# Low parts of weight chunks by an accumulating DMA, and the closing sums of an SSM scan on VectorE

## The chip, the cores and the metric

The kernel runs on one core of one Trainium2 chip, with its TensorE (matrix products), VectorE, ScalarE, GpSimd and SyncE, a 128-partition on-chip memory and 16 DMA engines. The metric is the device time of one execution in microseconds; lower is better. In the profile the engines are called PE (with PEld for its weight loads), DVE, ACT, POOL and SP; a q behind the name (SPq, POOLq) is the engine's queue of instructions that only issue or wait.

## What is computed

One layer of a decoder block for 256 tokens of 2048 columns, in float32:

```python
u = RMSNorm(h)
q, k, v, s_in, g_a, g_s = split(u @ w_in)             # 1024, 1024, 1024, 1024, 2048, 2048 columns
y_a = diff_attention(q, k, v)                         # 8 heads, two softmax maps each
y_s = s5(s_in)                                        # 64 groups, complex state of 64, scan over tokens
y_s = gelu(y_s); y_s = y_s * sigmoid(y_s @ w_glu + b_glu)
merged = sigmoid(g_a) * (y_a @ Wa) + sigmoid(g_s) * (y_s @ Ws)
h = h + RMSNorm(merged @ w_out)
z = RMSNorm(h)
h = h + RMSNorm((silu(z @ w_gate) * (z @ w_up)) @ w_down)
```

## The kernel before

**Split products.** Each float32 weight and each activation is kept as a high part (rounded to the format float32r of TensorE) and a low part (what the rounding left). A product is three matmuls: x high by w high, x high by w low, x low by w high.

**Blocks and chunks.** The weights stream through in blocks. A block is 16 or 8 chunks of 128 rows by 1024 columns (512 KB). For a chunk there are 4 products of 128x512 (2 token tiles by 2 halves of the columns), so 12 matmuls. The blocks run in the order ssm (the SSM's input), q, k, v, ga0, ga1, wa0, wa1, gs0, gs1, then glu, ws0, ws1, wo0, wo1, eleven ffn blocks and down.

**The ring.** `do_load` (L178) loads a chunk on SP's queue into `raw`, of which there are 4 buffers. `do_split` (L191) makes `hi` with a copy on ScalarE (L205) and `lo` with a subtraction on VectorE (L206); there are 3 buffers each of `hi` and `lo` until the glu block. `ensure` (L210) writes the split of a chunk two chunks ahead of its matmuls and the loads a further four ahead. A load waits until its raw buffer is free, that is until `lo` of the chunk that held it has been made.

**Side work.** `prep` (the parameters of the SSM), `u_parts`, `ssm` and `attn` are Python generators in a list of tasks. After the matmuls of a chunk `pump` (L230) takes as much from them as the budget SIDE = 1.4 allows. The SSM works through 16 halves of groups (the loop at L723). For each half GpSimd builds the rotation tables tabC and tabS of the next one (six instructions, L635 to L640); TensorE brings B u into `side`; VectorE rotates it (ssA to ssD), scans it (four scans, L756 and L757) and rotates it back (four products, L762 to L767); GpSimd closes with a difference into `sre` (L764) and a sum into `sim` (L768). TensorE then multiplies these with C (`finish`, L672). The next half reuses ssA to ssD.

**The order.** Until the second chunk of the first block the instructions stay in the order of the program (`pin`). After that a scheduler that simulates the times when the kernel is built decides the order on each engine and puts in the waits; on the chip each engine then follows its fixed order. GpSimd also issues the DMAs of its own queue, in the same order as its other work.

**Memory.** `big8` (L142) gives tiles of 128x2048 from a pool of 6. `bb` holds the SSM's B in `prep` (L567 to L613) in two tiles of the pool mixp.

Of the kernel before, what the change touches and what calls it, by code (L numbers as in the profile page):

```python
# [9 lines left out]
F32 = mybir.dt.float32  # L10
# [16 lines left out]

SIDE = 1.4     # how much of the side work goes between two chunks of weights


class InOrder:
    """An engine whose instructions stay in the order of the program while pin[0] is set."""

# [12 lines left out]
class Block:  # L46
    """One pass of a weight stripe (nk k-tiles of 1024 columns) through the tensor engine."""

    def __init__(self, name, nk, load, lhs, evac, order=None, pre=None, post=None,
                 budget=0.0, alloc=None, mm=None, ensure=None, before=None):  # L50
        self.name, self.nk, self.load, self.lhs, self.evac = name, nk, load, lhs, evac
        self.order, self.pre, self.post, self.budget = order, pre, post, budget
        self.alloc, self.mm, self.ensure = alloc, mm, ensure
        self.before = before or {}


# [12 lines left out]
def token_order(nk, head=0, tail=0):  # L69
    """Token tile 0 before token tile 1 over the first `head` and the last `tail` chunks."""  # L70
    steps = []
    if head:
        for t in range(2):
            for k in range(head):
                steps.append([(k, t, c) for c in range(2)])
    else:
        steps.append([(0, t, c) for t in range(2) for c in range(2)])
        head = 1
    for k in range(head, nk - tail):
        steps.append([(k, t, c) for t in range(2) for c in range(2)])  # L80
    for t in range(2):
        if tail:
            for c in range(2):
                steps.append([(k, t, c) for k in range(nk - tail, nk)])
    return steps
# [3 lines left out]
def hybrid_block_kernel(  # L89
# [45 lines left out]
    def side4():  # L135
        """One bank out of the four, where nothing else needs two at once."""
        cyc["n"] += 1
        if cyc["n"] % 4 == 3:
            cyc["t"] = side2()
        return side() if cyc["n"] % 4 in (1, 2) else cyc["t"][:, 1 if cyc["n"] % 4 == 0 else 0, :]  # L140
# [7 lines left out]
    class Scratch:  # L148
        """Short-lived tiles, cut from a few of the large ones."""

# [21 lines left out]

# [1 line left out]
    flat = []  # L174
# [3 lines left out]
    def do_load(i):  # L178
        """Loads one chunk; late in the kernel some go in pairs into spare large tiles."""
        blk, k = flat[i]  # L180
        if late.get("ffn") and i % 8 in (4, 6):
            r = big8(shape=(P, 2, 1024))
            blk.load(k, r)
            raws[i], raws[i + 1] = r[:, 0, :], r[:, 1, :]
            return 2
        r = ring.tile([P, 1, 1024], F32, tag="raw", name=nm("raw"), bufs=4)
        blk.load(k, r)
        raws[i] = r[:, 0, :]
        return 1

    def do_split(i):  # L191
        blk, k = flat[i]
        if late and i % 5 >= 3:
            h = late["pool"].tile([P, 1024], F32R, tag="hi", name=nm("hi"), bufs=2)
            l = late["pool"].tile([P, 1024], F32R, tag="lo", name=nm("lo"), bufs=2)
        else:
            h = ring.tile([P, 1024], F32R, tag="hi", name=nm("hi"), bufs=3)
            l = ring.tile([P, 1024], F32R, tag="lo", name=nm("lo"), bufs=3)
        if i == 0:
            first_split(h, l, raws.pop(0))  # L200
            his[i], los[i] = h, l
            return
        if blk.ensure:
            blk.ensure(k)
        A.copy(h, raws[i])  # L205
        V.tensor_tensor(l, raws[i], h.bitcast(F32), op=ALU.subtract)  # L206
        his[i], los[i] = h, l
        del raws[i]
# [10 lines left out]
    def cap(blk, n, start=False):  # L219
        """The splits go no further than n chunks from the start of blk, for now."""  # L220
        state["cap"] = None if n is None else blk.base + n
# [89 lines left out]

# [1 line left out]
    ident = const.tile([P, P], F32, name="ident")  # L313
# [8 lines left out]

# [1 line left out]
    xT_h = tpool.tile([P, 16, S], F32R, tag="T16", name="xT_h")  # L324
# [29 lines left out]
    def warm_up(n):  # L354
        """Products without a use, which bring the tensor engine's clock up while the first data comes in."""
        for _ in range(n):
# [36 lines left out]
    def make_rstd(ss, n, tag, inv):  # L393
        """(sum of squares * inv + eps) ** -0.5 for [P, n]."""
        ms = const.tile([P, n], F32, name=nm(tag + "m"))
# [17 lines left out]

# [1 line left out]
    def dve_exp(dst, src, n, pool):  # L415
# [13 lines left out]
    def dve_sincos(s_out, c_out, th, n, pool):  # L429
# [32 lines left out]
        V.tensor_copy(nn, q.bitcast(I32))  # L462
        # quarter turns: cos = [1,0,-1,0], sin = [0,1,0,-1]
        V.tensor_scalar(a, nn, 2.0, None, op0=ALU.is_equal)
# [11 lines left out]

# [1 line left out]
    def prep():  # L478
# [36 lines left out]
        yield 2.0  # L515
        # -(exp(s1) - exp(s2) + lam_init)
        nlam = const.tile([P, 1], F32, name="nlam")
# [20 lines left out]
        yield from dve_sincos(fl(sn), fl(cs), fl(th), 256, pp)  # L538
        # coef = (a_bar - 1) / lam
        w = [pp.tile([P, 32], F32, name=nm("cw")) for _ in range(6)]  # L540
# [16 lines left out]
        yield 1.5  # L557
        # b_bar, [ (g p), h, pair ] from transposes of the rows
        bps = []
        for t_ in braw:  # L560
# [5 lines left out]
            yield 0.5  # L566
        bb = [mixp.tile([P, 32, 16], F32, name=nm("bb")) for _ in range(2)]  # L567
        bc = lambda c_: c_.unsqueeze(1).broadcast_to([P, 16, 32])
        tmp = [pp.tile([P, 16, 32], F32, name=nm("bt")) for _ in range(2)]
        for o, (c0, c1, op) in enumerate(((cre, cim, ALU.subtract), (cim, cre, ALU.add))):  # L570
# [3 lines left out]
            yield 1.8  # L574
        # rotation tables: e^{i theta b}, b < 16, and e^{i theta 16 a}, a < 16
        tabs = []
# [27 lines left out]
        yield 0.1  # L604
        # B as blocks for pairs of groups, transposed, in high and low parts
        bh, bl = (ga[:, i, :, :].rearrange("p a (c o q) -> p (a c) o q", c=4, o=2) for i in range(2))
# [18 lines left out]

# [1 line left out]
    def table(hh):  # L627
# [16 lines left out]
    def u_parts():  # L644
        """u transposed, and its high and low parts to where the products take them from."""
        un = hold["u"]
# [21 lines left out]
    def ssm():  # L668
# [38 lines left out]
        def bu_mm(hf):  # L707
            # u and B of two pairs of groups: [u high; u low; u high] against [B high; B high; B low]
            us, bs = hold.pop("stack")
# [13 lines left out]
        for hh in range(2 * NG):  # L723
# [39 lines left out]
            V.tensor_tensor(tC, tD, tss, op=ALU.mult)  # L763
            G.tensor_tensor(sre[:, 2 * hf:2 * hf + 2, :], tA, tC, op=ALU.subtract)  # L764
            yield 1.2
            V.tensor_tensor(tB, tB, tss, op=ALU.mult)
            V.tensor_tensor(tD, tD, tcs, op=ALU.mult)  # L767
            G.tensor_tensor(sim[:, 2 * hf:2 * hf + 2, :], tB, tD, op=ALU.add)  # L768
            yield 1.2
# [7 lines left out]
        for k in range(8):  # L777
            tc.keep_in_program_order(A.activation(uT[:, k, :], uT[:, k, :], AF.Gelu_apprx_tanh))
            yield 0.1
        # the table of the sigmoids that come next is loaded ahead of them  # L780
        tc.keep_in_program_order(A.activation(const.tile([P, 1], F32, name="presig"), half[:, :1], AF.Sigmoid))
# [4 lines left out]

# [1 line left out]
    def attn():  # L788
# [113 lines left out]

# [1 line left out]
    def lhs_of(th, tl):  # L904
# [32 lines left out]
    def first_split(h, l, raw):  # L937
        """The first chunk and the first two k-tiles of x, in the order in which they are used."""
        ps = x_transposes(0)
# [10 lines left out]

    # first block: transposes of x run one step ahead of their use
    xdone = [1]
# [74 lines left out]

    # GLU: the weights are stationary, so that the result comes out transposed
    def glu_pre():
# [53 lines left out]
    def m_transpose(hf):  # L1083
        """Transposes of the merged branches for one half of the columns."""
        if not mT:
# [142 lines left out]

# [1 line left out]
    def lz(k, t):  # L1230
# [52 lines left out]

    # the rest of the norm, four k-tiles of one token tile at a time, ahead of their use
    blocks[-NB].before = {
# [13 lines left out]

    # down: k-tile by k-tile, 2048 columns, all banks  # L1300
    hs = {}
# [32 lines left out]
    def dn_evac(key, accs):  # L1334
        # the two banks of one tile are read only once both are complete
        t, c = key
# [25 lines left out]
    def dn_finish(t, c0, n, eng=None):  # L1362
        """The last scaling, the residual and the store of n columns."""
        f, r, cs = hold["f"][t], hold["rf", t], slice(c0, c0 + n)
# [60 lines left out]
```

## Time and profile before

| what | value |
|---|---|
| median of the runs | 1446.54 us (1445.51 to 1448.1, 3 runs) |
| span of the profiled execution | 1444.7 us |
| PE busy | 1384.3 us, 96% of the span |
| DVE busy | 912.6 us, 63% |
| ACT busy | 670.7 us, 46% |
| POOL busy | 279.8 us, 19% |
| DMA moved | 266.69 MB, 185 GB/s in the mean |

The profiled execution lasted its span and what lies around it: the first instruction starts when the span starts, and the median of the runs is 1.8 us above the span. Matmuls overlap in TensorE's pipeline, so its busy time says only where it has nothing to do at all. The shares are means over stages with different limits; views of single stretches, given in microseconds from the start of the span, tell them apart. A granted clock of 1.00 is 2.4 GHz.

### The profile page before, as it was taken

What the parts mean: (1) busy time and instruction counts of PE and PEld (TensorE: products, weight loads), DVE (VectorE), ACT (ScalarE), POOL (GpSimd) and SP (SyncE); (2) the same over time, 40 slices, a digit from 0 to 9 for tenths busy, and PEclk for the clock granted to TensorE, in tenths of its full rate; (3) what the DMA queues carried; (4) which work ended last, traced back from release to release, by engine and by line L of the source; (5) the groups of instructions that cost most, each with busy time, mean ns of one, the idle gap of its engine ahead of it and who ended that gap; (6) DMA issues with size and microseconds to landing.
All of it is one profiled execution on the core that took longest, in us unless ns stands there. A gap on an engine that the chain in (4) does not pass through costs nothing.

```text
span 1444.7 us, 17345 instructions
## 1 busy us (share of the span) xinstructions
PE 1384.3 (96%) x6367; PEld 1123.6 (78%) x6367; DVE 912.6 (63%) x1114; ACT 670.7 (46%) x963; POOL 279.8 (19%) x227
## 2 busy tenths in 40 slices
PE   8999897899889899999999999999999999999997
PEld 6887665678667579888788888888888888888885
DVE  5965889978898876755764444444444445555555
ACT  4654343375533356444464444444444444444443
POOL 3293676501756620000000000000000000000001
PEclk9999899999989899999999999999999999999999
DMA  8688554445455466655576556466565555555651
GB/s 259 187 265 256 159 153 124 133 147 165 142 153 153 118 187 234 248 189 191 164 258 219 174 190 201 161 207 203 172 205 169 198 203 177 204 191 188 203 175 59
DMA packets 102005, 266.69 MB, mean 185 GB/s; under 512 B 10176, under 2 KB 17168, under 8 KB 98528
## 3 DMA queue, kind: packets, MB, share of 16 engines
q1 hardware_dynamic: 100704, 260.09, 55.7%
q10 hardware_dynamic: 608, 4.20, 0.8%
q0 software_dynamic: 608, 1.30, 0.4%
q8 instruction: 50, 0.82, 0.2%
q14 instruction: 35, 0.29, 0.1%
HBM read 257.16 MB, written 8.39 MB: 184 GB/s over the span
## 4 chain that ended last, share of the span: by engine, by line
issue 52%; PE 29%; DVE 11%; POOL 5%; DMA 1%; ACT 1%; SPq 0%; POOLq 0%; DVEq 0%; ACTq 0%
PE acc L41 27%; PE side L41 3%; DVE lo L41 3%; POOL sre L764 2%; DVE ssC L41 2%; DVE ssB L41 2%; DVE ssD L41 2%; DVE ssA L41 2%; POOL sim L768 1%; POOL tabS L638 1%; DMA b<-in_x_dram 1%; ACT hi L41 1%; DMA raw<-in_w_in_dram 0%; DVE b L41 0%; SPq L623 0%
## 5 line engine op out<-in xcount | busy, mean ns | idle before, releaser
L41 DVE TENSOR_TENSOR lo<-raw,hi 128x1024 fp32r<-128x1024 f32 (+1 forms) x341 | 439.2, 1294 | 242.5 <-ACT hi L41 237.5
L41 ACT CAST hi<-raw 128x1024 fp32r<-128x1024 f32 (+1 forms) x340 | 354.7, 1051 | 406.4 <-PE acc L41 327.1
L41 PE MATMUL acc<-lo,zT_h 128*128 128x512 f32 x704 | 274.9, 390 | 0.0
L41 PE MATMUL acc<-hi,zT_l 128*128 128x512 f32 x704 | 274.0, 389 | 0.0
L41 PE MATMUL acc<-hi,zT_h 128*128 128x512 f32 x704 | 270.9, 392 | 0.2 <-ACT zT_h L41 0.2
L41 DVE TENSOR_TENSOR lo<-b,hi 128x1024 fp32r<-128x1024 f32 x124 | 151.1, 1224 | 147.6 <-ACT hi L41 147.6
L41 PE MATMUL acc<-lo,xT_h 128*128 128x512 f32 x512 | 211.8, 417 | 15.6 <-DVE lo L41 15.6
L41 PE MATMUL acc<-hi,xT_l 128*128 128x512 f32 x512 | 207.1, 407 | 0.0
L41 ACT CAST hi<-b 128x1024 fp32r<-128x1024 f32 x124 | 130.5, 1053 | 120.4 <-PE acc L41 104.0
L41 PE MATMUL acc<-hi,xT_h 128*128 128x512 f32 x512 | 169.7, 411 | 3.9 <-ACT hi L41 3.5
L41 PEld LDWEIGHTS acc<-hi,zT_h 128*128 128x128 f32 x704 | 132.2, 188 | 27.7 <-ACT zT_h L41 0.7
L41 PEld LDWEIGHTS acc<-hi,zT_l 128*128 128x128 f32 x704 | 132.2, 188 | 27.6
L41 PEld LDWEIGHTS acc<-lo,zT_h 128*128 128x128 f32 x704 | 132.2, 188 | 26.6
L41 PEld LDWEIGHTS acc<-lo,xT_h 128*128 128x128 f32 x512 | 102.0, 199 | 43.7 <-DVE lo L41 21.0
L398 POOL TENSOR_TENSOR rstdf<-rstdfm,half 128x1 f32<-128x1 f32 x2 | 1.1, 546 | 691.6 <-DVE rstdfm L41 691.6
L41 PEld LDWEIGHTS acc<-hi,xT_h 128*128 128x128 f32 x512 | 99.3, 197 | 28.6 <-ACT hi L41 4.9
L41 PEld LDWEIGHTS acc<-hi,xT_l 128*128 128x128 f32 x512 | 101.7, 199 | 21.5 <-issue 0.8
L41 PE MATMUL acc<-hi,b 128*128 128x512 f32 x256 | 84.2, 404 | 0.8 <-DVE ga L41 0.6
L764 POOL TENSOR_TENSOR sre<-ssA,ssC 128x512 f32<-128x512 f32 x16 | 47.5, 2970 | 121.1 <-DVE ssC L41 121.1
L41 PE MATMUL acc<-lo,hTh 128*128 128x512 f32 x176 | 68.5, 389 | 0.0
L41 PE MATMUL side<-hi,hTh 128*128 128x512 f32 x176 | 68.5, 389 | 0.0
L41 PE MATMUL side<-lo,hTh 128*128 128x512 f32 x176 | 68.5, 389 | 0.0
(209 smaller groups left out, 1818.0 us busy)
## 6 DMA issues: line engine op xcount, KB each, us to landing
raw<-in_w_in_dram SPq DMA_DIRECT2D x127, 512.0 KB, 4.2
raw<-in_w_ffn_gate_dram SPq DMA_DIRECT2D x96, 256.0 KB, 2.8
raw<-in_w_ffn_up_dram SPq DMA_DIRECT2D x96, 256.0 KB, 3.0
raw<-in_w_ffn_down_dram SPq DMA_DIRECT2D x44, 512.0 KB, 3.7
b<-in_w_ffn_down_dram SPq DMA_DIRECT2D x22, 1024.0 KB, 4.9
b<-in_w_ffn_gate_dram SPq DMA_DIRECT2D x40, 512.0 KB, 3.8
b<-in_w_ffn_up_dram SPq DMA_DIRECT2D x40, 512.0 KB, 4.8
raw<-in_w_out_dram SPq DMA_DIRECT2D x32, 512.0 KB, 4.6
```

Of the source, the lines that this page charges most:

```text
L41: ins = f(*a, **kw)
L398: G.tensor_tensor(r, ms, half[:, :n], op=ALU.pow)
L638: G.tensor_tensor(tss, hi(sa), lo(cb), op=ALU.mult)
L764: G.tensor_tensor(sre[:, 2 * hf:2 * hf + 2, :], tA, tC, op=ALU.subtract)
L768: G.tensor_tensor(sim[:, 2 * hf:2 * hf + 2, :], tB, tD, op=ALU.add)
```

## The change

In the blocks q, k, v, ga, wa and gs each odd chunk gets its low part without VectorE. ScalarE makes hi as before, and it also writes minus the rounded weights into `lo`. A DMA on GpSimd's queue then adds `raw` to `lo` in place. `lo` of each fourth chunk (k % 4 == 3) has a buffer of its own, lo4. `bb` moves into a tile of `big8`, which frees the room for lo4. The two closing sums of the SSM's loop move from GpSimd to VectorE. Apart from comments that are dropped, this is all:

```diff
@@ class Block
+        self.dma_lo = name[:2] in ("q", "k", "v", "ga", "wa", "gs")
@@ do_split
             h = ring.tile([P, 1024], F32R, tag="hi", name=nm("hi"), bufs=3)
-            l = ring.tile([P, 1024], F32R, tag="lo", name=nm("lo"), bufs=3)
+            l = (small([P, 1024], "lo4", F32R) if blk.dma_lo and k % 4 == 3 else
+                 ring.tile([P, 1024], F32R, tag="lo", name=nm("lo"), bufs=3))
...
         A.copy(h, raws[i])
-        V.tensor_tensor(l, raws[i], h.bitcast(F32), op=ALU.subtract)
+        if blk.dma_lo and k % 2:
+
+            A.mul(l, raws[i], -1.0)
+            G.dma_start(l.bitcast(F32), raws[i], accum_op=ALU.add)
+        else:
+            V.tensor_tensor(l, raws[i], h.bitcast(F32), op=ALU.subtract)
         his[i], los[i] = h, l
         del raws[i]
@@ prep
-        bb = [mixp.tile([P, 32, 16], F32, name=nm("bb")) for _ in range(2)]
+        bb_ = big8()
+        bb = [bb_[:, 1024 * i:1024 * i + 512].rearrange("p (a h) -> p a h", a=32) for i in range(2)]
@@ ssm
-            G.tensor_tensor(sre[:, 2 * hf:2 * hf + 2, :], tA, tC, op=ALU.subtract)
+            V.tensor_tensor(sre[:, 2 * hf:2 * hf + 2, :], tA, tC, op=ALU.subtract)
...
-            G.tensor_tensor(sim[:, 2 * hf:2 * hf + 2, :], tB, tD, op=ALU.add)
+            V.tensor_tensor(sim[:, 2 * hf:2 * hf + 2, :], tB, tD, op=ALU.add)
```

## Rows read from the trace of the kernel before

**Rows 1.** Head of the page.

```profile
span 1444.7 us, 17345 instructions
```

**Rows 2.** Stretches: length; PE, PEld, DVE, ACT, POOL busy (count); clock, DMA share, GB/s.

```profile
60.00:525.00 465.00, 419.78 (x1938) 325.11 (x1937) 386.79 (x512) 216.25 (x392) 258.50 (x183) 0.94 0.55 164
109.00:525.00 416.00, 370.78 (x1692) 284.42 (x1691) 351.32 (x465) 186.72 (x332) 216.85 (x129) 0.93 0.52 156
...
60.00:109.00 49.00, 49.00 (x248) 40.70 (x247) 35.47 (x48) 29.54 (x61) 41.65 (x55) 1.00 0.76 234
109.00:135.00 26.00, 22.45 (x90) 17.86 (x89) 12.87 (x10) 13.09 (x25) 11.63 (x7) 0.87 0.91 266
...
166.00:233.00 67.00, 57.79 (x242) 42.19 (x241) 59.42 (x69) 23.78 (x35) 46.99 (x27) 0.88 0.51 155
...
800.00:1000.00 200.00, 200.00 (x901) 165.53 (x900) 94.12 (x81) 87.29 (x90) 0.00 (x0) 1.00 0.57 190
```

**Rows 3.** Chain of waits, 166 to 233 us: shares by line, two pieces (start, us).

```profile
by line: issue 18.6%; POOL sre L764 15.1%; DVE lo L41 10.6%; POOL sim L768 10.0%; PE acc L41 9.6%; DVE ssD L41 8.4%; DVE ssB L41 7.8%; DVE ssA L41 7.5%; DVE ssC L41 7.4%; POOL tabS L638 4.7%; PE side L41 2.5%; DVE b L41 0.8%; POOLq L764 0.1
...
169.17 3.39 POOL sre L764
...
193.52 2.24 POOL sim L768
```

**Rows 4.** Who waited for whom, whole span: us in total, times, longest.

```profile
PE acc L41 <- DVE lo L41: 19.7, 11, 3.0
...
DVE ssA L41 <- POOL sre L764: 14.9, 11, 3.2
...
DVE ssB L41 <- POOL sim L768: 10.0, 9, 1.2
```

**Rows 5.** Groups on POOL, 345 to 525 us: count, busy, mean ns, idle before.

```profile
L764 POOL TENSOR_TENSOR sre<-ssA,ssC 128x512 f32<-128x512 f32 x9 | 26.0, 2887 | 60.1 <-DVE ssC L41 60.1
```

**Rows 6.** Instructions on lo alone, one stretch: PE, PEld, DVE; clock, DMA.

```profile
60.00:525.00 465.00, 204.34 (x487) 97.29 (x487) 171.54 (x122) 0.94 0.55 164
```

**Rows 7.** Groups of the whole span: count, busy us, mean ns, idle before.

```profile
L41 ACT CAST hi<-raw 128x1024 fp32r<-128x1024 f32 (+1 forms) x340 | 354.7, 1051 | 406.4 <-PE acc L41 327.1 <-DMA raw<-in_w_ffn_up_dram 21.0 <-DMA raw<-in_w_in_dram 17.2
...
L764 POOL TENSOR_TENSOR sre<-ssA,ssC 128x512 f32<-128x512 f32 x16 | 47.5, 2970 | 121.1 <-DVE ssC L41 121.1
...
L640 POOL TENSOR_TENSOR tabS<-tabS,tabt 128x512 f32<-128x512 f32 x16 | 27.6, 1726 | 1.3
...
L41 DVE TENSOR_TENSOR ssC<-ssC,ssD 128x512 f32<-128x512 f32 x16 | 22.3, 1391 | 0.0
...
L635 POOL TENSOR_TENSOR tabC<-tabc,tabc 128x512 f32<-128x512 f32 x16 | 21.8, 1365 | 0.0
...
L41 DVE TENSOR_TENSOR ssD<-ssD,tabC 128x512 f32<-128x512 f32 x16 | 10.9, 680 | 0.0
```

**Rows 8.** DMA issues: count, KB each, median us from issue to landing.

```profile
raw<-in_w_in_dram SPq DMA_DIRECT2D x127, 512.0 KB, 4.2
...
b<-in_w_ffn_down_dram SPq DMA_DIRECT2D x22, 1024.0 KB, 4.9
...
cn<-in_ssm_c_im_dram POOLq DMA_DIRECT2D x1, 256.0 KB, 12.8
...
subw<-in_subln_w_dram POOLq DMA_DIRECT2D x1, 64.0 KB, 5.6
```

**Rows 9.** Timeline of POOL, 5 to 19 us: start, duration, instruction.

```profile
5.65 0.95 POOL L492 DMA_DIRECT2D cn<-in_ssm_c_re_dram  x1
...
15.93 0.53 POOL L499 DMA_DIRECT2D subw<-in_subln_w_dram  x1 [1.05 <-DMA b<-in_ssm_b_im_dram]
```

**Rows 10.** Who SP's queue waited for, 60 to 525 us: total, times, longest.

```profile
SPq L308 <- DVE lo L41: 334.7, 104, 9.2
```

## The prediction

> **What bounds the kernel now.** I read the page first, then the stretches by block, then the chain of waits inside one stretch, then who waited for whom. The profiled execution spans 1444.7 us [rows 1]. Late in the kernel TensorE is the limit: between 800 and 1000 us it issues 901 matmuls in 200 us at clock 1.00 with no idle time, 0.222 us each, so one chunk of weights (12 matmuls) takes 2.66 us there [rows 2]. The change touches the blocks q to gs1, which run from 60 to 525 us, 122 chunks in 465 us [rows 2, 6], 3.8 us a chunk. From 109 us on TensorE is busy 370.8 of 416 us, so 45.2 us are idle, and the granted clock averages 0.93, between its levels of 2.4 and 1.2 GHz: 0.07 x 416 = 29 us more at most [rows 2]. Together 74 us are the most that any relief in this stretch can give back. In the first of these blocks, 60 to 109 us, TensorE never idles and the clock is 1.00: nothing is to be had there.
>
> What ends last there is VectorE together with GpSimd. In the v block (166 to 233 us) VectorE is busy 59.4 of 67 us [rows 2]; the chain through that stretch lies on VectorE for some 42% (lo, ssA to ssD), on GpSimd's closing sums sre and sim for 25%, on TensorE for 12% [rows 3]. TensorE waits 19.7 us for lo and VectorE 24.9 us for the two sums (14.9 for sre, 10.0 for sim) [rows 4]. So two things are late: the subtraction that makes lo, and the step of the SSM loop that goes to GpSimd and back.
>
> **The SSM loop.** Half of a group is one loop. From 345 to 525 us there are 9 in 180 us, 20 us each, some 5.2 chunks [rows 5]. Sixteen run in all; two fall into the attention stretch or the start, 14 keep this pace.
>
> **Part 1, lo off VectorE.** 122 instructions of lo take 171.5 us in 60 to 525 us, 1.41 us each [rows 6]. The odd chunks of q, k, v, ga, wa and gs are 24+16+8+16 = 64, so 64 x 1.41 = 90 us leave VectorE; per loop 2.6 x 1.41 = 3.7 us. ScalarE gets 64 scaled copies; the cast to hi is the nearest row, 1.05 us, so 67 us [rows 7]. It is busy 216 of 465 us [rows 2], would be at 61%, and its main idle time is waiting for TensorE, so I cost this at nothing; if its cover went, it is 1.05 us on the path of an odd chunk.
>
> **Part 2, sums on VectorE.** 32 sums. VectorE's 128x512 op on two SBUF tiles took 0.68 us undisturbed (ssD) and 1.39 us beside GpSimd (ssC) [rows 7]; I take 0.9, since GpSimd loses the sums but keeps the tables: 1.8 us per loop, 29 us in all. In return the chain loses sre's 3.4 us and sim's 2.24 us [rows 3], the 24.9 us of waiting go, and GpSimd loses about 80 us (16 x 2.97 us for sre, and sim) [rows 7]. VectorE's 20 us loop becomes 20 - 1.6 (waits) - 3.7 + 1.8 = 16.5 us, less where GpSimd no longer disturbs it, say 16. What is late next is TensorE: 5.2 x 2.66 = 13.8 us of chunk matmuls plus about 2 us of side products, 16 us. Gross gain: 14 x 4 = 56 us, inside the 74.
>
> **Part 3, the accumulating DMA.** No row shows one. Three prices are unknown; each is added work, so none is below nothing.
> (a) Its time from issue to landing. Below: a 512 KB load lands in 4.2 us and a 1 MB one in 4.9, so a second pass over 512 KB adds 0.7. Above: the 256 KB load of cn on GpSimd's queue took 12.8 us, in a crowd and in short rows; 64 KB of subw took 5.6 [rows 8]. I take 6 to 7, nearest to the 5.6 of the same queue plus the larger size.
> (b) GpSimd's issue. 0.53 us for subw's 128 rows, 0.95 us for cn [rows 9]; I take 0.6, 38 us in all, less than the sums free. But the queue is in order: an issue waits behind the table of the next half (six instructions of 1.37 to 1.73 us, 9.1 us [rows 7]) and the next table, or attention's pow (L877), behind an issue that waits for ScalarE. In a 16 us loop GpSimd is in the table over half of the time, so an issue waits some 0.55 x 4.5 = 2.5 us on average and 9 at worst.
> (c) The DMA engines' time. From 800 to 1000 us a share of 0.57 carries 190 GB/s, so 512 KB fills the 16 engines for 1.57 us [rows 2]. An accumulate reads two operands and writes one: one pass (1.57 us), two (3.15) or three (4.7). I take about 2.3, 1.5 passes, because one side of a pass can overlap the other's.
>
> Does (a) fit? A lo buffer now comes back after four chunks (three rotating ones and the new lo4), 4 x 3.1 = 12.5 us at the new pace. The scaled copy reads raw alone, so it can start before hi has a buffer. Copy 1.05, wait 2.5, issue 0.6, landing 6.5 make 10.7 us; TensorE then holds it for 1 to 3 us. It is tight. raw has four buffers too, and loads already wait for lo 104 times [rows 10]; an odd raw is now held until the DMA lands, and behind its next load, in SP's order, stand the loads of later chunks and the u and B fetches. I charge 18 to 20 us: each third odd chunk (about 20) late by 1 us, past what TensorE can do meanwhile with hi. And I charge 12 us for the q block and the head of k, where DMA is at 0.76 and 0.91 already [rows 2]: 49 x 0.76 + 26 x 0.91 = 61 us of 75, and 11 accumulates add 17 to 52 us; at 2.3 us, 25, making 86, 11 over.
>
> bb now lies in one of the six large tiles until the B blocks are made; it ends before q's first output needs a tile. Nothing.
>
> **Sum.** 56 - 20 - 12 = 24 us: span 1444.7 to 1420.7. The median of the runs, 1446.5, stands 1.8 us above the span, so 1422.
>
> **A page beside the rows.** On (a): the Trainium skill ("DMA: Bandwidth & Descriptors", Anatomy of one DMA) fits a GpSimd-issued DMA as 2.0 us plus bytes over 436 GB/s, 3.2 us for 512 KB, an estimate from that page. The row of the same queue, 5.6 us for 64 KB [rows 8], is far above it. By the page the low parts would always be in time, and the sum would be that of rival 1.
>
> **Rivals.**
> 1. All transfers hide: the waiting time is covered by TensorE taking hi products first, and the early stretch stays as it is. Then 56 us are kept: 1391. For it: ScalarE can copy early, the loads land well ahead. Against: the 12.5 us loop of a lo buffer, the table in front of an issue.
> 2. The DMA engines become the bound in q to gs1. They are busy 0.55 x 465 = 256 us [rows 2]. At two passes 64 x 3.15 = 202 us come on top, 458. The crowded stretch from 109 to 135 us held a share of 0.91 [rows 2]; at that share they take 458/0.91 = 503 us, 38 more than now: 1484. At three passes, 612, and 1594 if nothing overlaps. It decides from (465 x 0.91 - 256)/64 = 2.6 us of engine time per accumulate; a late lo then also drops the clock. For it: the share is already high early. Against: a read in SBUF may be shorter than one in HBM, and the 0.91 is no hard limit. The Trainium skill ("Collectives: The Full Stack", The bandwidth ceiling) says that an add in a DMA is slow through its two source reads, not through the add, and gives half a copy's rate. By it two passes hold, and so this rival's 1484; no row of before shows it.
> 3. It does not do what it says: the order that the scheduler draws up puts the scaled copy behind hi on ScalarE, or the issue behind each table, and the wait for VectorE's lo becomes an equal one for the DMA's: 24 us more late time, 1446.
>
> **How the numbers follow.** Forecast 0.41 (its own range 1405 to 1440), rival 1 0.13, rival 2 0.35, rival 3 with what lies near it 0.11. Faster by over 0.2% (about what a measurement of this kernel tells from no change) is 0.41 + 0.13 + 0.02 of the last = 0.56; same 0.09; slower 0.35. Both signs hold much of the chance, so the range goes from 1392, which leaves out half of rival 1, to 1486, which takes in rival 2 at two passes but not three. The predicted time is the likeliest case's, 1422.
>
> **What would show it.** Right: 64 fewer lo on VectorE, 64 DMAs from raw to lo land in 6 to 7 us; GpSimd's sre and sim are gone and VectorE no longer waits for GpSimd there; loops of 16 to 18 us; TensorE idle in 109 to 525 us well under 45 us; DMA share between 0.75 and 0.9. Wrong: TensorE's waits for lo now end with that DMA and sum to more than 45 us, the share stands at 0.95, or landings exceed 10 us (rival 2); GpSimd's DMA issues wait for ScalarE, or stand behind L635 to L640, with the share moderate (rival 3); landings under 5 us and idle under 15 us (rival 1).

## The result: slower by 13 us

| kernel | median of the runs | span of the profiled execution |
|---|---|---|
| before | 1446.99 us (1445.51 to 1448.10, 4 runs) | 1444.7 us |
| after | 1459.66 us (1457.15 to 1462.79, 4 runs) | 1458.5 us |

Here and below, before and after name the two kernels. The ratio is 1.009 (95% interval 1.0074 to 1.0106). The forecast was 1422 us, faster by 24; the time lies in the range given, on the other side of no change.

The same stretches as before the change (columns as in [rows 2]: length; PE, PEld, DVE, ACT, POOL busy with counts; clock, DMA share, GB/s):

```profile
60.00:109.00 49.00, 41.56 (x193) 32.80 (x193) 20.82 (x34) 28.15 (x50) 39.31 (x63) 0.90 0.93 246
109.00:135.00 26.00, 23.45 (x91) 18.30 (x91) 7.82 (x7) 16.34 (x34) 9.21 (x8) 0.86 0.94 237
109.00:525.00 416.00, 371.16 (x1703) 280.99 (x1703) 317.02 (x445) 238.20 (x399) 192.08 (x149) 0.94 0.85 223
60.00:525.00 465.00, 412.72 (x1896) 313.79 (x1896) 337.84 (x479) 266.36 (x448) 231.40 (x211) 0.93 0.86 226
166.00:233.00 67.00, 59.74 (x265) 43.55 (x265) 66.48 (x79) 34.43 (x49) 48.34 (x34) 0.95 0.80 214
```

VectorE lost 49 us of work between 60 and 525 us and GpSimd 27, and yet TensorE issued 42 matmuls fewer there, 1896 for 1938 [rows 2]. The loss starts at once: between 60 and 109 us, where TensorE had been busy all the time at clock 1.00, it is now busy 41.6 of 49 us at 0.90, and the DMA engines stand at 0.93. From 109 us on its idle time is 44.8 us, as before (45.2). Between 166 and 233 us VectorE is still full, 66.5 of 67 us, with half of its subtractions gone.

Who waits for whom in after (us in total, times, longest):

```profile
POOL lo L211 <- ACT lo L41: 151.2, 31, 21.3
...
PE acc L41 <- DMA lo<-raw: 25.3, 14, 4.3
...
PE acc L41 <- ACT hi L41: 8.2, 3, 5.0
PE acc L41 <- DVE lo L41: 6.9, 8, 2.2
```

VectorE's 24.9 us of waiting for the sums [rows 4] are gone, and TensorE's wait for VectorE's lo fell from 19.7 us [rows 4] to 6.9. In their place it waits 25.3 us for the accumulating DMA and 8.2 us for hi. SP's queue (60 to 560 us) now waits for that DMA more than for VectorE, which it had waited for in before [rows 10]:

```profile
SPq L315 <- DMA lo<-raw: 231.2, 53, 7.8
SPq L315 <- DVE lo L41: 108.4, 39, 7.8
```

The new operations on the page of after: GpSimd's queue in the list of queues (packets, MB, share of 16 engines), then two groups (count | busy us, mean ns | idle before), then the issues (count, KB, median us to landing):

```profile
q0 software_dynamic: 9824, 34.85, 13.0%
...
L41 ACT ACTIVATE lo<-raw 128x1024 fp32r<-128x1024 f32 x64 | 67.9, 1060 | 56.9 <-DMA raw<-in_w_in_dram 28.6
L211 POOL DMA_DIRECT2D lo<-raw x64 | 55.8, 872 | 177.8 <-ACT lo L41 151.2
...
raw<-in_w_in_dram SPq DMA_DIRECT2D x127, 512.0 KB, 4.9
lo<-raw POOLq DMA_DIRECT2D x64, 512.0 KB, 6.1
```

In before the queue q0 held 0.4%. So 64 accumulates cost 12.6% of 1458.5 us, 2.87 us of all 16 engines each; that is called the engine time of a transfer here. The scaled copy takes 1.06 us, the issue 0.87 us, the landing 6.1 us.

### The profile page after: what moved, and what is told of

The parts are those of the page before. It is cut to its first block, busy times and chain, and to the rows that moved or that the text cites. A ratio compares the mean times of both kernels' runs of the same rounds, so it can differ in the third digit from the quotient of the medians.

```text
span 1458.5 us, 17513 instructions
## 1 busy us (share of the span) xinstructions
PE 1389.7 (95%) x6367; PEld 1122.4 (77%) x6367; DVE 861.7 (59%) x1082; ACT 729.5 (50%) x1027; POOL 254.5 (17%) x259
## 4 chain that ended last, share of the span: by engine, by line
issue 50%; PE 25%; DVE 13%; DMA 6%; SPq 2%; ACT 1%; POOL 1%; POOLq 0%; DVEq 0%; ACTq 0%
PE acc L41 23%; DVE ssB L41 3%; DVE lo L41 3%; DMA raw<-in_w_in_dram 3%; DMA lo<-raw 3%; PE side L41 3%; DVE ssC L41 2%; DVE ssA L41 2%; DVE ssD L41 2%; SPq L631 1%; DVE sim L41 1%; SPq L673 1%; DVE sre L41 1%; ACT hi L41 1%; ACT lo L41 0%
## 5 line engine op out<-in xcount | busy, mean ns | idle before, releaser
L41 DVE TENSOR_TENSOR lo<-raw,hi 128x1024 fp32r<-128x1024 f32 (+1 forms) x277 | 351.6, 1273 | 293.7 <-ACT hi L41 288.5
L41 PE MATMUL acc<-hi,xT_h 128*128 128x512 f32 x512 | 174.4, 411 | 12.1 <-ACT hi L41 8.2
L41 ACT ACTIVATE lo<-raw 128x1024 fp32r<-128x1024 f32 x64 | 67.9, 1060 | 56.9 <-DMA raw<-in_w_in_dram 28.6
L211 POOL DMA_DIRECT2D lo<-raw x64 | 55.8, 872 | 177.8 <-ACT lo L41 151.2
```

What stands on the lines that cost most here:

```text
L41: ins = f(*a, **kw)
L211: G.dma_start(l.bitcast(F32), raws[i], accum_op=ALU.add)
```

## The experiments

Two theories of the loss. **A**: the accumulates' engine time; the crowd that it makes delays loads and other transfers, whatever waits for the low parts. **B**: the round of a low part through its buffers (load, copy, GpSimd, landing, TensorE) is too long. Beside them stands the question whether the gross gain was there at all. The ratios are to the kernel before on the same chip. One limit holds for all but two of the comparisons: the scheduler draws up a new order of instructions for a version, so the order changes along with what the edit changes. The two exceptions, both with plain copies, are named.

### The two halves of the change

**Sums alone**: before, with

```diff
-            G.tensor_tensor(sre[:, 2 * hf:2 * hf + 2, :], tA, tC, op=ALU.subtract)
+            V.tensor_tensor(sre[:, 2 * hf:2 * hf + 2, :], tA, tC, op=ALU.subtract)
```

and the same for sim.

> The kernel before with the two closing sums alone on VectorE, no accumulating DMA. Theory A (the DMA engines are what the change ran into: 2.9 us of engine time per accumulate, a share of 0.97 from 120 to 180 us): the sums are not to blame; the loop drops from 20 to some 18 us, VectorE's 25 us of waiting for GpSimd go, its own 29 us come: 1432 to 1446 us. Theory B (the loss is latency: ScalarE's copy, GpSimd's queue and the landing one after the other): the same as A here. Theory C (VectorE, full in the SSM stretch, can't take 32 more instructions): 1455 to 1465 us, most of the change's loss.

Measured: 1434.56 us, ratio 0.9911 (0.9894 to 0.9927). **DMA alone**: after, with the two sums back on GpSimd.

> The changed kernel with the sums back on GpSimd: the accumulating DMA alone. A: the crowd in the q and k blocks stays (26 us over before), the loops stay at 18 to 20 us: 1462 to 1475 us. B: GpSimd's queue is now longer by 80 us of sums, issues wait more, 1470 to 1490 us. C: without the sums the change gains, 1430 to 1446 us.

Measured: 1470.74 us, ratio 1.0161 (1.0144 to 1.0179). The sums gain 13 us, the low parts by DMA lose 23 to 25, and the two nearly add up.

### The gross gain by itself

```diff
             A.mul(l, raws[i], -1.0)
-            G.dma_start(l.bitcast(F32), raws[i], accum_op=ALU.add)
```

> The changed kernel without the accumulating DMAs: ScalarE writes minus the rounded weights and nothing is added to them, so the low part of each odd chunk of q, k, v, ga, wa and gs is left wrong. What is left is the relief of VectorE (64 subtractions) and the closing sums on it. The prediction's step (14 loops of 4 us): 1391 us. Rival (the loops get shorter by those 4 us but carry fewer chunks, since VectorE stays full in them, and only the chunks after the last loop run at TensorE's pace): 1412 to 1422 us.

Measured: 1422.46 us, ratio 0.9827 (0.9809 to 0.9844). With no price for a DMA at all the change gains 25 us, not 56, and so the DMAs cost 1459.7 - 1422.5 = 37 us (32 were charged). Against the sums alone, 64 subtractions fewer (90 us of VectorE [rows 6], with 64 scaled copies on ScalarE in their place) gain 12 us.

Where they gain them is seen at the end of gs1, the last of the changed blocks (start of its last matmul with lo, and of the first matmul of glu, in us of the profiled execution):

| version | last of gs1 | first of glu |
|---|---|---|
| before | 543.1 | 543.5 |
| sums alone | 523.5 | 531.1 |
| after without the DMAs | 520.1 | 520.8 |
| after | 556.7 | 557.3 |
| accumulates in q and k alone (below) | 535.1 | 535.5 |
| accumulates in v, ga, wa and gs alone (below) | 539.4 | 540.3 |
| dummy transfers (below) | 562.0 | 562.4 |
| dummies in v, ga, wa and gs alone (below) | 544.8 | 545.3 |

From the first matmul of glu to the end all of them take 901 to 902 us, only the sums alone 904. So what the change does is done by then, and the sums alone lose some 9 us at this one place: glu multiplies what the SSM has made, and there TensorE, through with gs1, waits for it.

```profile
531.15 0.80 PE L41 MATMUL acc<-b,hi 128*128 128x256 f32 x2 [7.02 <-ACT b L41]
```

The clock is 0.84 from 523.9 to 556.9 us then. Of the 12 us, 3.4 are thus gained in the blocks, and most of the rest because the SSM is done earlier (its last loop starts at 470.0 us, for 503.0) and glu needn't wait.

Why so little in the blocks? The instructions on the tile lo over five SSM loops (from one ssA<-side,tabC to the fifth after it) in before, sums alone, without DMAs, and after. TensorE, first in the list, makes four matmuls with lo for a chunk, so its count over four is the number of chunks:

```profile
409.69:509.47 99.78, 41.99 (x96) 20.08 (x96) 36.27 (x25) 0.90 0.47 139
```

```profile
403.12:503.00 99.88, 47.18 (x116) 21.85 (x115) 43.32 (x29) 0.98 0.55 164
```

```profile
390.18:470.04 79.86, 36.00 (x88) 17.26 (x88) 17.86 (x11) 11.82 (x12) 0.96 0.51 160
```

```profile
403.28:490.31 87.03, 36.73 (x87) 17.61 (x87) 17.40 (x11) 11.65 (x11) 9.65 (x11) 0.93 0.87 230
```

A loop of before takes 20.0 us and carries 4.8 chunks, 4.16 us a chunk. With the sums alone it still takes 20.0 us but carries 5.8: 3.44 us a chunk. Without VectorE's odd low parts it takes 16.0 us, as forecast, but carries 4.4: 3.63 us a chunk. The freed time of VectorE made the SSM run ahead of the chunks, and no chunk faster. In those loops VectorE stays the full engine: between 189.08 and 235.15 us, three loops of the version without DMAs, it works without a gap while TensorE stands for 8.5 us, and in the five loops above it is busy 79.55 of 79.86 us (all instructions; columns as in [rows 2]):

```profile
189.08:235.15 46.07, 37.55 (x176) 26.34 (x174) 46.07 (x57) 23.98 (x33) 29.24 (x19) 0.97 0.46 145
390.18:470.04 79.86, 73.27 (x334) 55.35 (x331) 79.55 (x102) 41.09 (x54) 45.90 (x28) 0.96 0.51 160
```

Two pieces of its timeline (start, us, instruction), VectorE's and then TensorE's:

```profile
212.84 1.74 DVE L41 TENSOR_TENSOR_SCAN ssB<-rr,ssA 128x256 f32<-128x256 f32 x2
214.50 1.24 DVE L41 TENSOR_TENSOR_SCAN ssD<-rr,ssC 128x256 f32<-128x256 f32 x2
215.66 1.19 DVE L41 TENSOR_TENSOR lo<-raw,hi 128x1024 fp32r<-128x1024 f32 x1
```

```profile
213.24 1.09 PE L41 MATMUL acc<-hi,xT_h 128*128 128x512 f32 x4
216.91 0.50 PE L41 MATMUL acc<-lo,xT_h 128*128 128x512 f32 x1 [2.58 <-DVE lo L41]
```

The next lo of an even chunk stands behind the scans in VectorE's order, and TensorE waits 2.58 us for it, odd chunks or no. Only the chunks that are left when the SSM has ended run at TensorE's pace.

### Engine time

**Plain copy**: after, where the DMA copies raw over lo in place of adding to it, so that these low parts hold the whole weights.

```diff
-            G.dma_start(l.bitcast(F32), raws[i], accum_op=ALU.add)
+            G.dma_start(l.bitcast(F32), raws[i])
```

> The changed kernel with a plain copy of raw into lo in place of the accumulating one, same queue, bytes, waits and buffers; the part of the product with lo of the odd chunks is left wrong. It measures what the addition (its second read) costs. A: engine time per DMA drops from 2.9 us to 1.3 to 1.7, the share from 60 to 556 us from 0.87 to about 0.7, landings from 6.1 to 4.5 us, time 1435 to 1447 us. B: the chain copy, queue, landing is shorter by 1 to 1.5 us only, time 1452 to 1458 us.

Measured: 1439.86 us, ratio 0.9946 (0.9931 to 0.9961). Its queue and its landing:

```profile
q0 software_dynamic: 9824, 34.85, 6.4%
...
lo<-raw POOLq DMA_DIRECT2D x64, 512.0 KB, 4.5
```

(6.4 - 0.4)% of 1438.5 us over 64 is 1.35 us of engine time, and the accumulate's 2.87 is 2.13 times that. Above the version without DMAs the plain copies cost 17.4 us (86 us of engine time) and the accumulates 37.2 us (184): 0.20 us of the kernel for a us of engine time in both. On each engine the instructions come in the same order as in after, so this comparison is free of the scheduler. But the landing is shorter too, and the run alone doesn't part A from B. The next runs bear on that.

**Dummy transfers**: sums on VectorE, all low parts by VectorE, and for each odd chunk two plain 512 KB DMAs that nobody waits for.

```diff
+        if blk.dma_lo and k % 2:
+            d = dsrc[0][:, k // 2 % 2, :]
+            A.copy(d[:, 0:1], h[:, 0:1].bitcast(F32))
+            for n in range(2):
+                G.dma_start(extra[:, i % 8 * 2 + n, :].rearrange("p (a b) -> p a b", a=2),
+                            d.unsqueeze(1).broadcast_to([P, 2, 512]))
```

> The kernel before with the sums on VectorE and every low part made by VectorE, and besides, for each odd chunk of q, k, v, ga, wa and gs, two plain DMAs of 512 KB on GpSimd's queue from a spare tile to DRAM, for which nothing waits: 128 transfers, some 2.7 to 3 us of engine time per odd chunk, as much as one accumulate takes. Theory A (the DMA engines' time is what the accumulates cost): 1434.6 plus the 23 us or so that they cost, 1452 to 1462 us. Theory B (the time of the chain of one low part through the buffers is what they cost): 1434 to 1442 us, with a DMA share near 0.86 in 60 to 560 us all the same. Between: both, and the excess over 1434.6 is A's part.

Measured: 1467.79 us, ratio 1.0142 (1.0125 to 1.0159); 1.40 us of engine time each, 2.8 for an odd chunk, at a DMA share of 0.86 between 60 and 560 us. That is 33 us over the sums alone, with no low part behind any DMA: theory A, though the run overshot A's own bound of 1462.

**Dummies in v, ga, wa and gs alone**, by the names in that condition.

> The sums on VectorE, every low part by VectorE, and the dummy transfers (two plain 512 KB DMAs for an odd chunk, nothing waits for them) in v, ga, wa and gs alone, 96 transfers. Theory A (engine time is the price in the late blocks too): some 15 to 20 of the 33 us that the dummies cost in all blocks, 1446 to 1456 us. Theory B (the round of a low part through its buffers is the price there): 1434 to 1441 us, at a DMA share of 0.75 to 0.85 from 240 to 560 us.

Measured: 1448.76 us, ratio 1.0004 (0.9995 to 1.0013). That is 14 us over the sums alone, A again.

Not all of the 33 and the 14 is traffic. The spare tile is cleared on GpSimd at the very start, the identity matrix that TensorE needs is made there at 9.9 us, for 2.1 in the sums alone, and TensorE waits; by 60 us it has issued 54 matmuls with lo, for 60 in the sums alone (first the sums alone, then the late dummies, whose first transfer starts at 172 us):

```profile
0.00:60.00 60.00, 22.93 (x60) 12.04 (x60) 20.84 (x18) 0.94 0.75 229
```

```profile
0.00:60.00 60.00, 19.92 (x54) 10.55 (x54) 18.57 (x17) 1.00 0.74 216
...
10.29 0.28 PE L41 MATMUL side<-ident,wrow 16*128 16x16 f32 x1 [6.95 <-POOL ident masks.py:199]
```

That is 1.5 chunks, some 4 us, and 3 with the dummies in all blocks (56 matmuls). So the traffic makes about 30 of the 33 us, and about 10 of the 14. At the end of gs1, where no wait of glu hides anything, it is 562.0 - 523.5 - 3 = 35 us for all dummies and 544.8 - 523.5 - 4 = 17 for the late ones; the accumulates themselves move that end by 556.7 - 520.1 = 37 us, and the late ones alone by 539.4 - 523.5 = 16 against the sums alone. The dummies are not the accumulates in every way: they write to DRAM, their issues take GpSimd 93.9 us in all (55.8 for the accumulates), and the order is another.

### Where the crowd hits

Accumulates **in q and k alone**, and **in v, ga, wa and gs alone**, each by this line of the changed kernel:

```diff
-        self.dma_lo = name[:2] in ("q", "k", "v", "ga", "wa", "gs")
+        self.dma_lo = name[:2] in ("q", "k")
```

> The changed kernel with the accumulating DMA in the blocks q and k alone (16 accumulates). Theory A (engine time in the crowded stretch carries the loss): over the 1434.6 us of the version with the sums alone, the 25 us of the whole change less the 10 that the late blocks cost by themselves, so 1446 to 1458 us, q ends near 124 us and k near 192, and the later blocks run as with the sums alone. The prediction's own step charged 12 us: 1447. Theory B (the late blocks' rounds carry it): 1435 to 1442 us.

> The changed kernel with the accumulating DMA in v, ga, wa and gs alone; q and k make lo on VectorE as before (48 - 8 = 40 + 8 accumulates less 16: 48 remain). A: the 26 us of q and k come back, the end of k is at 166 us again, and the later 13 us of gain stay: 1430 to 1438 us. B: a quarter of the accumulates goes, and with it a quarter of the late time: 1450 to 1456 us. C: 1455 us or more.

Measured: q and k alone 1440.03 us, ratio 0.9946 (0.9926 to 0.9966), 5 us over the sums alone; the late blocks alone 1444.40 us, ratio 0.9982 (0.9965 to 0.9998), 10 over them. Together they cost 25, not 15. The instructions on lo show why; first the sums alone, then q and k alone, then after:

```profile
60.00:225.00 165.00, 79.39 (x196) 37.91 (x196) 69.22 (x48) 0.97 0.70 209
225.00:500.00 275.00, 118.42 (x288) 55.55 (x288) 102.15 (x73) 0.97 0.49 150
```

```profile
60.00:225.00 165.00, 68.14 (x159) 32.54 (x158) 35.35 (x23) 15.32 (x15) 13.06 (x15) 0.89 0.85 230
225.00:500.00 275.00, 123.63 (x306) 58.38 (x306) 104.23 (x77) 0.00 (x0) 0.00 (x0) 0.99 0.52 158
```

```profile
60.00:225.00 165.00, 66.84 (x154) 31.95 (x155) 30.95 (x19) 19.07 (x18) 16.53 (x19) 0.89 0.90 234
225.00:500.00 275.00, 117.75 (x283) 55.64 (x282) 50.63 (x36) 38.18 (x36) 31.51 (x36) 0.96 0.83 218
```

By 225 us accumulates in q and k have cost 37 of TensorE's matmuls with lo, 9 chunks. The version with q and k alone regains 4.5 of them by 500 us; after regains none, at a DMA share of 0.83 in its late blocks. And the sums alone are a baseline that hides a part: at the end of gs1 q and k alone stand 535.1 - 523.5 = 12 us behind them and the late blocks alone 16, which together is 28 of after's 33. But the sums alone lose some 9 us there in waiting for the SSM, which the others don't, and so only 5 and 10 us show in the medians.

What happens in q and k is seen in SP's order. First the version without DMAs, then after, in the k block (start, us, issues of SP's queue):

```profile
117.19 11.48 SPq L630 DMA_DIRECT2D stack_b<-ga  x12
```

```profile
117.89 4.80 SPq L315 DMA_DIRECT2D raw<-in_w_in_dram  x3
123.38 18.41 SPq L631 DMA_DIRECT2D stack_b<-ga  x12
141.90 2.88 SPq L315 DMA_DIRECT2D raw<-in_w_in_dram  x3
```

Twelve writes of B in short rows take SP 0.96 us each in the quiet kernel, 1.53 us in after (and 0.96 again where q and k have no accumulates). From 123.4 to 141.9 us no load of a chunk is issued, and TensorE then waits for hi:

```profile
149.06 1.22 PE L41 MATMUL acc<-hi,xT_h 128*128 128x512 f32 x2 [4.99 <-ACT hi L41]
```

The dummies do the same to the writes of u (eleven in a row, 1.74 us each; 0.95 without DMAs):

```profile
81.95 19.19 SPq L678 DMA_DIRECT2D stack_u<-b  x11
```

### The round of a low part

**One step more**: after, with a GpSimd operation between the copy and the DMA.

```diff
+            G.tensor_scalar(l[:, :512], l[:, :512].bitcast(F32), 1.0, None, op0=ALU.mult)
```

> The changed kernel with one more GpSimd instruction (times 1.0 on half of lo, in place) between ScalarE's copy and each accumulate: 0.6 to 1.5 us more latency for each of the 64, no more engine time for the DMAs. A: DMA engines set the pace, 1457 to 1463 us, as the change. B: each odd chunk is late by that much more, 64 x 0.6 to 1.5 us less what is covered: 1475 to 1510 us.

Measured: 1505.38 us, ratio 1.0396 (1.0364 to 1.0429), with the DMA share down to 0.80 and TensorE's wait for the low parts up to 46.7 us. **Without lo4**, and **without lo4 but with five raw buffers** (two in place of three of each transposed tile of the last block pay for them):

```diff
-            l = (small([P, 1024], "lo4", F32R) if blk.dma_lo and k % 4 == 3 else
-                 ring.tile([P, 1024], F32R, tag="lo", name=nm("lo"), bufs=3))
+            l = ring.tile([P, 1024], F32R, tag="lo", name=nm("lo"), bufs=3)
```

> The changed kernel without lo4: all low parts rotate through the three buffers of the ring, so that a scaled copy can start one chunk later. A: 1457 to 1466 us. B: the accumulate starts up to 3 us later in each odd chunk: 1480 to 1530 us.

> As e14 (no lo4), with a fifth raw buffer, paid for by one buffer less of each transposed tile in the last block. Theory B1 (the round of a raw buffer sets the pace: load, ScalarE copy, GpSimd issue, landing, next load): the round gets 5/4 as long a time, most of the 16 us that e14 lost against the changed kernel come back, 1455 to 1465 us. Theory B2 (the round of a lo buffer sets it: it is written, filled, used by TensorE, then free for the next copy): nothing changes, 1470 to 1480 us, and ScalarE's copies still wait some 70 us for TensorE. Theory A (engine time of the DMAs): nothing changes either, but the DMA share in 60 to 560 us stays at 0.84 to 0.86 with the copies not waiting.

Measured: 1475.60 us, ratio 1.0193 (1.0169 to 1.0217), and 1476.86 us, ratio 1.0205 (1.0171 to 1.0240). Without lo4 the waits are these:

```profile
ACT lo L41 <- PE acc L41: 71.4, 43, 6.2
PE acc L41 <- DMA lo<-raw: 54.3, 33, 4.7
```

So B is real as well: the round through a lo buffer has little slack in the changed kernel, and a longer round or a buffer fewer is paid for, while a fifth raw buffer gives nothing back. 46 us for one step more is partly GpSimd's own time: the added operation takes it 111 us in all, and how much of the 46 is that was not parted from the round. What traffic costs without any B (about 30 us for the dummies, 35 at the end of gs1) leaves little of the 37 us to B as the change stands; the two were not parted more finely.

### Fewer accumulates

Late blocks with **plain copies**, with **every fourth** chunk (k % 4 == 3, which lo4 holds), and with **every third** (k % 3 == 2, lo4 for each second of these); all blocks with **every fourth**:

```diff
-        if blk.dma_lo and k % 2:
+        if blk.dma_lo and k % 4 == 3:
```

> The kernel of e3_late_blocks (v, ga, wa, gs) with plain copies in place of the accumulating ones; the product with lo of those odd chunks is left wrong. e3 measured 1444.4 us, e1 (sums alone) 1434.6. A (engine time of the accumulate: 2.9 us, of a plain copy 1.35): the share falls from 0.81 to below 0.7 and the time under e1, 1425 to 1434 us, since 48 x 1.3 us of VectorE are free and nothing is crowded. B (latency of copy, queue and landing): 1.5 us of 10 less, 1438 to 1443 us.

> The kernel of e3_late_blocks with each fourth chunk only (k % 4 == 3, the one with the buffer of its own): 24 accumulates in place of 48. A: half of the engine time is added, 69 us, no stretch crowded: 1428 to 1438 us, at or under e1. B: half of the late parts, 1437 to 1441 us.

> As the version with every fourth chunk of v, ga, wa and gs (1425 us), but every third (k % 3 == 2), the own buffer for each second of these: some 30 accumulates in place of 24. If relief of VectorE still pays at this share: 1417 to 1423. If the engine time of 6 to 8 more accumulates (2.9 us each, 20 us) and rounds of the rotating buffers weigh as much as the relief: 1423 to 1433. With every second chunk it was 1444.

> The changed kernel with the accumulating DMA for every fourth chunk (k % 4 == 3) alone, in all of q, k, v, ga, wa and gs: 32 accumulates, each in the buffer of its own. Against the version with the fourth chunks of v, ga, wa and gs alone (1425 us) it adds 8 accumulates in the crowded blocks q and k. Theory A: 8 times 2.87 us, 23 us of engine time in a stretch at a share of 0.92 to 0.97, so 15 to 25 us, 1440 to 1450. Theory B: only one landing under way in four chunks and no rotating buffer held by it, so 0 to 8 us, 1425 to 1433.

| accumulates | where | median | ratio (95%) |
|---|---|---|---|
| 48 plain copies | late blocks | 1424.05 | 0.9846 (0.9819 to 0.9873) |
| 24 | late blocks, every 4th | 1425.21 | 0.9852 (0.9827 to 0.9876) |
| 29 | late blocks, every 3rd | 1433.94 | 0.9904 (0.9887 to 0.9921) |
| 48 | late blocks, every 2nd | 1444.40 | 0.9982 (0.9965 to 0.9998) |
| 32 | all blocks, every 4th | 1442.21 | 0.9961 (0.9946 to 0.9975) |

Eight accumulates more, in the crowded q and k, cost 17 us: A's figure, though sixteen in q and k alone moved the end of gs1 by 12 only, so that what they cost hangs on what follows. The first row has the order of the fourth, on every engine, and is 20 us faster: the copies in place of the adds, with nothing else changed. In the late blocks every fourth chunk is the best of the three shares: TensorE waits 2.4 us for the DMA in all, and it gains 9 us over the sums alone, 4 of them by the end of gs1 (519.3 us for 523.5) and most of the rest because glu needn't wait. With the sums on VectorE it is the fastest version here that makes all low parts, 1425 us, and beats both kernels: 22 us under before and 34 under after.

## Why the prediction was wrong, step by step

**What bounds the kernel: right in part.** The sums and lo on VectorE were what ended last, and the waits for them went. Of the 74 us that any relief could give back, less than half comes even when the DMAs are left out; the version without them, 109 to 525 us:

```profile
109.00:525.00 416.00, 385.40 (x1830) 295.78 (x1829) 313.94 (x458) 260.59 (x427) 136.58 (x91) 0.97 0.54 168
```

TensorE's idle time falls from 45.2 to 30.6 us and its clock rises from 0.93 to 0.97, 0.04 x 416 = 17 us: 31 us together.

**The gross gain, 14 x 4 = 56 us: the step that failed.** It measures 25 us. The loop did shrink to 16.0 us. But it was counted at "5.2 chunks", the average pace of all the blocks; five late loops of before carry 4.8, and the shorter ones only 4.4, and three loops ahead of the attention (189.08 to 235.15 us) 43/4/3 = 3.6 for 4.4. What was missed is that time taken off the loop is a gain only for chunks that still ride in it: those left over run later at 2.66 us or more [rows 2]. The trace has the account. Starts of the sixteen loops (first and last), then the instructions on lo up to the last of them, for before and for the version without DMAs, and at the end what follows it there:

```profile
L41 DVE TENSOR_TENSOR ssA<-side,tabC x16: 675/692/694, 138.4 to 509.5; 128x512 f32<-128x512 f32 x16
L41 DVE TENSOR_TENSOR ssA<-side,tabC x16: 673/680/691, 147.8 to 470.0; 128x512 f32<-128x512 f32 x16
```

```profile
0.00:509.47 509.47, 219.96 (x528) 105.60 (x528) 186.81 (x135) 0.94 0.57 172
0.00:470.04 470.04, 204.72 (x505) 98.52 (x505) 101.78 (x73) 60.40 (x57) 0.96 0.59 181
470.04:521.00 50.96, 27.79 (x72) 13.35 (x72) 11.58 (x10) 7.39 (x7) 1.00 0.54 176
```

The last loop starts 39.5 us earlier, but with 23 matmuls with lo fewer behind it, 5.75 chunks. These run later at 2.8 us each (18 chunks in the 51 us that follow), 16 us, so 39.5 - 16 = 23 us are left, which is the 520.1 for 543.1 us at the end of gs1. The 15 steps from first to last loop did shrink by 49 us; the first loop starts 9.4 us later, with two chunks more done. It starts at 138.8 us, as before, where q and k are left on VectorE (accumulates in the late blocks alone), so the later start comes with the change in q and k, and not with bb, whose "nothing" holds. "Late next is TensorE" failed too: in the loops it is still VectorE.

**Part 2, the sums: right in direction.** The waits of 24.9 us [rows 4] went, and 13 us were gained with the sums alone, over half of the whole gross gain (20 us at the end of gs1, 543.1 to 523.5, before the wait of glu).

**Part 1, ScalarE at nothing: right.** From 60 to 525 us it is busy 266.4 of 465 us in after, 57% (61% was forecast).

**Part 3, (a) landing: right**, 6.1 us in the 6 to 7 taken. The Trainium skill ("DMA: Bandwidth & Descriptors", Anatomy of one DMA) would have it at 3.2 us; even the plain copy took 4.5, so here the page is too low and the rows of before were the better guide. **(b) GpSimd's issue: mis-sized**, 0.87 us for 0.6. Of the 64 issues 31 found GpSimd idle, waiting for ScalarE's copy (151.2 us in all); how long the others stood behind a table was not parted. So rival 3 holds in one thing, TensorE's wait for VectorE's lo (19.7 us) became a like one for the DMA's (25.3 us), but not in its condition, a moderate DMA share: it is 0.86. **(c) Engine time: mis-sized**, 2.87 us for 2.3, beyond the 2.6 from which rival 2 was to decide. It was taken at 1.5 passes for an overlap that no row showed; 2.87 us is 1.8 of the passes of 1.57 us. The Trainium skill ("Collectives: The Full Stack", The bandwidth ceiling) puts the add of a reducing collective at half a copy's rate for its two source reads; the trace agrees, 2.13 times the plain copy.

**The charges, 20 + 12 = 32 us: nearly right in sum**, 37 measured, but not in their places. The crowd in q and k was charged with 12 and late low parts with 20. By 225 us 9 chunks are lost there, some 9 x 3.4 = 31 us, of which 12 are left at the end of gs1 where the later blocks have no accumulates; and by the dummies traffic alone, with no low part late, makes most of the loss.

So even with the charges as forecast the right gross gain would have given 1446.5 - 25 + 32 = 1454 us. **Rival 2** had the mechanism, and by its own rule with the measured price (256 + 64 x 2.87) / 0.91 = 483 us, 18 more than 465, 1464 us; that this is near 1460 is partly luck, since it lets no gain stand and the share averaged 0.86, not 0.91.

## What to carry to other kernels

Before a relief of a full engine is counted, ask what will use the freed time: here VectorE's order let side work run ahead, and 90 us of it bought 12, most of them at one wait behind the blocks. A transfer that nothing waits for still has a price: over all 64 odd chunks some 0.2 us of the kernel for a us of engine time, where the DMA share without them was 0.54; 17 us for the 23 of eight more in q and k, where it was 0.76 and 0.91 [rows 2]. An accumulate costs two copies. And compare versions at the end of the stretch that was changed, too: a wait behind it can hide or add 9 us. Move work to DMA in a small share and where DMA is idle: 24 of the 64 gained 9 us where all 64 lost 25.

## What was not expected of the hardware

DMAs from one queue slow the issuing of another: SP's 256 KB writes in short rows went from 0.96 to 1.53 us each beside the accumulates (B), and from 0.95 to 1.74 us beside the dummies (u), and SP's later loads stood behind them. And an accumulate took GpSimd longer to issue than a plain 512 KB copy between the same tiles, 0.87 us for 0.59.
